# A hybrid encoder layer on one core: other DRAM layouts for operands, VectorE statistics for four tiles, a scheduling hint for the MLP residual, the last shifts on VectorE

## The chip, the cores and the metric

The kernel runs on one core of a Trainium2 chip. Five engines work side by side, each through its own queue in order: TensorE (PE, with its weight loads PEld), VectorE (DVE), ScalarE (ACT), GpSimd (POOL) and SyncE (SP, which here only issues DMAs). The metric is the device time of one execution in microseconds, lower is better.

## The reference, cut to what matters

One layer on 1024 tokens of 1024 channels, float32 in and out:

```
x   = layer_norm(x)
h   = x @ w_in                                   # 1024 x 3600
o_gdn = gated_delta(conv(h_qkv), decay, beta)    # chunked scan, both directions
o_na  = neighborhood_attention(q, k, v, rpb)     # 8 heads of 64, window 8 x 16, bias per offset
mix = concat(o_gdn, rms_norm(o_na)) @ w_out
x   = layer_norm(alpha * x + mix) * g1 + b1
ff  = square(relu(x @ w1 + b1)) @ w2 + b2        # 1024 -> 4096 -> 1024
out = layer_norm(alpha * x + ff) * g2 + b2'
```

## The kernel before, in words

Tokens are held as 8 tiles of 128. Each float32 matrix product is split into a high and a low part and takes three matmuls (hi x hi, hi x lo, lo x hi); the splits are a copy on ACT (or DVE) and a subtraction on DVE, the helper at L71. The program runs in stages:

- 0 to 60 us: x is loaded and normalised, the first projections start. Up to 400 us: the remaining w_in projections (`load_w`, one 512 KB column block of 128 channels per load), convolution and the delta-rule scan; 400 to 490 us: the projections of the attention heads (`na_v`, `na_qk`), woven with the last scan steps. `na_v` writes the values to a DRAM scratch `vs_d`.
- 490 to 680 us: attention, head by head. It loads queries and keys (L700, L704), values (`load_v`, L694, tile `vt`) and the position bias (`load_b`, L709, tile `B`). The scores are the matmuls `pss` (L735, L736); DVE adds the bias and takes the row maximum (`sn`, `nm`, L739); ACT takes the exponential; PE transposes and multiplies by the values (`po`, L754). In this stretch the queue of SP also loads the output weights (`woraw`) and the residual rows (`yacc`, L832).
- 680 to 715 us: the last part of the output projection (`psop`, L802 to L804). DVE adds it to `yacc` (L806 with a row sum, L809 without), `layer_norm` (L933 to L947) normalises each tile and stores it to the scratch `y_d`, PE transposes it (`psx`, L977) and ACT evacuates it (`x1f`, L981). The tiles go in two halves, `hf` 0 and 1, of four each.
- 715 to 1036 us: the upper MLP product by a Strassen-like scheme (`up_pair`, one pair of 128-column blocks g per call, products `psA`, `psB`, `psD`, ...). In it the weight sums of the second product are made as well: `w2_load` and `w2_sums` (L1033 to L1043) read w2 in 256 KB pieces, form four sums on DVE and store them to `t_d`. The activations and their sums go to `h_d` (256 KB per block, issued by ACT).
- 1036 to 1346 us: the lower MLP product, 7 products of 4 groups. For group n, `down_ops(n)` loads 1 MB of a left operand (`h_d`) and 1 MB of a right one (`t_d` or w2) into `d2r` (or `wraw` for every third n), and splits them by ACT L1184 and DVE L71. It is called two groups ahead of the matmuls `psdn` (`down_mm`, L1283 to L1285).
- `residual` (L1203 to L1210), called at group n = 1, loads the rows of `y_d` into `yr` and scales them. `take` adds the products to `yr`, and `finish` (L1220 to L1248) makes the last LayerNorm: tiles 4 to 7 in the middle of the seventh part, tiles 0 to 3 at the end, with `kind` 0 (tiles 0, 1), 1 (tile 2) or 2 (tile 3).

A scheduler sets the order of each engine's queue from its own estimate of the program, so one edit can move instructions far from it. Every hardware DMA of SP and ACT takes one of eight semaphores in turn, so it also waits until the eighth DMA before it, on either queue, has landed. `tc.issue_after(i)`, which the change uses, tells the scheduler to place an instruction behind `i`.

Of the kernel before, what the change touches and what calls it, by code (L numbers as in the profile page):

```python
# [15 lines left out]
P = 128  # L16
# [20 lines left out]
def tile_trunk(ctx: ExitStack, tc: tile.TileContext, A: dict, out: bass.AP):  # L37
# [378 lines left out]
    def decay_beta():  # L416
        wab_raw = p1.tile([P, NK, 16], F32, name="wab_raw")
        D.dma_start(wab_raw, A["w_in"][:, 2048:2064].rearrange("(kt p) c -> p kt c", p=P))
        wab = p1.tile([P, NK, 32], F32R, tag="iX", name="wab")
# [198 lines left out]
    ks_d = dr.tile([8, 2, 64, T], F32, name="ks_d")  # L618
    vs_d = dr.tile([4, 16, 32, 8, 64], F32, name="vs_d")
    starts = (0, 8, 24, 32)  # L620
    pace = pacer(steps, 300, 4)

    def na_qk(kind, p):
        hi, lo = load_w(2064 + (0 if kind == "q" else 512) + p * P, V)
        dst = qs_d if kind == "q" else ks_d
# [19 lines left out]
    def na_v(p):  # L645
        hi, lo = load_w(2064 + 1024 + p * P, V)
        for half in range(2):
            psj = ps_j("psv")
            gemm_x(psj, hi, lo, half, pace)
            vT = np_.tile([P, 512], F32, tag="nst", name="vT", bufs=4)  # L650
            S.activation(vT, psj, AF.Copy)
            ps = ps_j("pvt", (P, 4, P))
            for q in range(4):
                TE.transpose(ps[:, q], vT[:, q * P:(q + 1) * P], ident)
            st = np_.tile([P, 4, P], F32, tag="vst", name="vst", bufs=2)
            V.tensor_copy(st, ps)
            for e2 in range(2):
                for j in range(4):
                    p0 = e2 * 64 + starts[j]
                    D.dma_start(  # L660
                        vs_d[j, half * 8 + e2:half * 8 + e2 + 7:2, :, 2 * p:2 * p + 2, :]
                        .rearrange("r c h x -> c r (h x)"),
                        st[p0:p0 + 32])

# [226 lines left out]
    def w1_raw(g):  # L891
        raw = raw8().rearrange("p a (k c) -> p (a k) c", c=2 * P)
        D.dma_start(raw, A["w1"][:, g * 2 * P:(g + 1) * 2 * P].rearrange("(kt p) c -> p kt c", p=P))
        return raw

    def w_quad(raw, a, k):
        return raw[:, k * 4:k * 4 + 4, a * P:(a + 1) * P]

# [131 lines left out]
    def w2_load(g, hc):  # L1030
        r = w2p.tile([P, 2, 2, 256], F32, tag="r", name="w2r", bufs=2)
        for k in range(2):
            D.dma_start(r[:, k], A["w2"][(2 * g + k) * P:(2 * g + k + 1) * P, :]  # L1033
                        .rearrange("p (j c) -> p j c", j=2)[:, :, hc * 256:hc * 256 + 256])
        return r

    def w2_sums(g, hc, r):
# [24 lines left out]
    def up_pair(g, mid=None):  # L1062
# [58 lines left out]
        def join5(pe):  # L1121
            V.tensor_tensor(h22, u3, pe, ALU.add)  # L1122
            V.tensor_tensor(u2, u2, pe, ALU.add)
            act2(h22, h22, f + 1, h_d[2, g])
            step()
# [33 lines left out]
        for i, h in enumerate((s1, s2, s3, s4)):  # L1159
            S.dma_start(h_d[3 + i, g], h)  # L1160


    w2q = A["w2"].rearrange("(g k p) (j c) -> k j p g c", k=2, j=2, p=P)
    left = [h_d[i].rearrange("g p c -> p g c") for i in range(7)]
    right = [t_d[i].rearrange("g p c -> p g c") for i in range(4)]
    order = [(left[0], w2q[0, 0]), (left[4], right[1]), (left[5], right[2]), (left[3], right[0]),
# [53 lines left out]
    def finish(t, kind):  # L1220
# [16 lines left out]
        parts = ((0, 512), (512, 256), (768, 256)) if kind == 2 else ((0, 512), (512, 512))  # L1237
# [17 lines left out]
    def take(i, q, ps):  # L1255
# [19 lines left out]
        elif i == 5:  # L1275
            add(y0[:, lo_], y0[:, lo_], ps)
            stats(q, 0, 512)

    def down_mm(ps, n, q, c, start, stop):
        h, w = ops2[n]  # L1280
        qs_ = slice(q * P, (q + 1) * P)
        for k in range(4):
            TE.matmul(ps, h[:, 0, k, qs_], w[:, 0, k, c], start=(start and k == 0), stop=False)  # L1283
            TE.matmul(ps, h[:, 0, k, qs_], w[:, 1, k, c], start=False, stop=False)  # L1284
            TE.matmul(ps, h[:, 1, k, qs_], w[:, 0, k, c], start=False, stop=(stop and k == 3))  # L1285

# [37 lines left out]
def prepare(inputs):  # L1324
# [32 lines left out]
    def col(x, n):  # L1357
        return C(x.reshape(n, P).T)

    gb = [np.broadcast_to(a[k][0][:, None, :], (2, 8, 4)).reshape(64) for k in ("dt_bias", "a_log")]  # L1360
    d = {
# [5 lines left out]
        "ln_in_b": a["ln_in_b"].reshape(1, DM),  # L1367
        "w_in": a["w_in"][0],
# [4 lines left out]
        "rpbT": C(tab[:, idx]),  # L1373
        "w_out": a["w_out"][0],
# [29 lines left out]
```

## Time and profile before

| what | value |
|---|---|
| median of 3 runs | 1366.89 us (1367.37, 1366.89, 1360.23) |
| profiled execution | 1359.64 us, its span 1357.9 us |
| PE busy | 1288.7 us (95%) |
| DVE / ACT / POOL busy | 933.3 (69%) / 647.0 (48%) / 188.6 us (14%) |
| granted TensorE clock | 0.981 of full speed |
| DMA | 242690 packets, 268.32 MB, 198 GB/s over the span |
| packets under 512 B / 2 KB / 8 KB | 38928 / 171920 / 242592 |

The span runs from the first to the last instruction; the 1.7 us that the execution took beyond it lie around it. PE busy counts matmuls with modelled ends, so that 95% says how often PE had one to do, not how fast it was.

### The profile page before, as it was taken

How to read it: one execution, taken by the hardware profiler on the slowest of the kernel's cores; microseconds unless marked ns; L12 is line 12 of the kernel's file. 1: busy time of each engine (PE TensorE's matmuls, PEld its weight loads, DVE VectorE, ACT ScalarE, POOL GpSimd, SP SyncE). 2: the span in 40 equal slices, each digit the busy share in tenths (PEclk: the TensorE clock that was granted, in tenths of full speed). 3: DMA queues.
4: the chain of work that ended last, by engine and by line, in shares of the span. 5: the costliest groups of instructions: out<-in, count | busy, mean ns of one | idle time of the engine just before them, and what ended most of it. 6: DMA issues, size and time to landing. Idle time of an engine off the chain costs nothing.

```text
span 1357.9 us, 20075 instructions
## 1 busy us (share of the span) xinstructions
PE 1288.7 (95%) x7318; PEld 1073.8 (79%) x7318; DVE 933.3 (69%) x1707; ACT 647.0 (48%) x1256; POOL 188.6 (14%) x216
## 2 busy tenths in 40 slices
PE   5999999999999987899989899999999999999996
PEld 3688888887889876788867788888887888888885
DVE  6755797852247835757659988878885695565856
ACT  5457666433433136345487465445454533333532
POOL 3000001011103316913230000000000000000403
PEclk8999999998999998999998999999999999999998
DMA  6224638466877499955154786787779955556621
GB/s 196 52 82 125 157 102 170 134 156 185 254 214 218 138 263 319 244 167 154 51 180 146 226 298 218 266 286 254 251 268 379 379 196 187 190 185 219 252 83 63
DMA packets 242690, 268.32 MB, mean 198 GB/s; under 512 B 38928, under 2 KB 171920, under 8 KB 242592
## 3 DMA queue, kind: packets, MB, share of 16 engines
q1 hardware_dynamic: 208416, 216.70, 52.4%
q10 hardware_dynamic: 34176, 50.34, 10.6%
q8 instruction: 58, 0.95, 0.3%
q14 instruction: 40, 0.33, 0.1%
HBM read 181.99 MB, written 85.00 MB: 197 GB/s over the span
## 4 chain that ended last, share of the span: by engine, by line
PE 58%; DVE 5%; DMA 3%; ACT 2%; issue 1%; POOL 1%; SPq 0%; DVEq 0%; ACTq 0%
PE psdn L1283 7%; PE psdn L1284 7%; PE psdn L1285 7%; PE po L754 2%; PE psop L802 2%; PE psop L803 2%; PE psop L804 2%; PE psA L931 2%; PE psA L929 2%; PE psA L930 2%; PE psD L929 1%; PE psD L931 1%; PE psD L930 1%; PE psB L929 1%; PE psB L931 1%; PE psB L930 1%
## 5 line engine op out<-in xcount | busy, mean ns | idle before, releaser
L1283 PE MATMUL psdn<-d,d 128*128 128x512 f32 (+1 forms) x464 | 175.6, 385 | 2.9 <-ACT d L1184 2.9
L1284 PE MATMUL psdn<-d,d 128*128 128x512 f32 (+1 forms) x464 | 176.9, 382 | 0.0
L1285 PE MATMUL psdn<-d,d 128*128 128x512 f32 (+1 forms) x464 | 176.9, 382 | 0.0
L71 DVE TENSOR_TENSOR d<-d2r,d 128x1024 fp32r<-128x1024 f32 x72 | 85.9, 1239 | 65.3 <-ACT d L1184 60.6
L1184 ACT ACTIVATE d<-d2r 128x1024 fp32r<-128x1024 f32 x72 | 71.3, 1049 | 115.6 <-PE psdn L1285 92.9
L1283 PEld LDWEIGHTS psdn<-d,d 128*128 128x128 f32 x464 | 87.8, 190 | 20.4 <-ACT d L1184 3.3
L1285 PEld LDWEIGHTS psdn<-d,d 128*128 128x128 f32 x464 | 87.4, 188 | 17.1
L1284 PEld LDWEIGHTS psdn<-d,d 128*128 128x128 f32 x464 | 87.5, 189 | 16.8
L93 POOL TENSOR_TENSOR lrs<-lrs,mhalf 128x1 f32<-128x1 f32 x8 | 6.5, 808 | 600.7 <-DMA d2r<-h_d 546.3
L120 PE MATMUL psj<-xlo,whi 128*128 128x512 f32 x192 | 77.6, 404 | 2.6 <-DVE xlo L71 2.6
L119 PE MATMUL psj<-xhi,whi 128*128 128x512 f32 x192 | 77.0, 402 | 0.7 <-DVE xhi L170 0.7
L121 PE MATMUL psj<-xhi,wlo 128*128 128x512 f32 x192 | 76.5, 399 | 0.0
L71 DVE TENSOR_TENSOR d<-wraw,d 128x1024 fp32r<-128x1024 f32 x40 | 47.8, 1234 | 27.7 <-ACT d L1184 27.7
L71 DVE TENSOR_TENSOR wlo<-wraw,whi 128x1024 fp32r<-128x1024 f32 x28 | 34.2, 1223 | 46.6 <-ACT whi L110 41.9
L240 DVE SCALAR_TENSOR_TENSOR cy<-hraw,convw,cy 128x1024 f32<-128x1024 f32 x48 | 61.2, 1280 | 5.6 <-ACT cy L238 4.5
L887 ACT ACTIVATE w1t<-ws 128x512 fp32r<-128x512 f32 x64 | 39.6, 627 | 52.4 <-PE psE L931 7.8
L1057 ACT ACTIVATE h<-h,b1T 128x512 f32<-128x512 f32 x48 | 34.6, 720 | 62.9 <-DVE h L1122 31.2
L1184 ACT ACTIVATE d<-wraw 128x1024 fp32r<-128x1024 f32 x40 | 39.9, 1048 | 49.4 <-PE psdn L1285 41.5
L754 PEld LDWEIGHTS po<-vt,et 128*128 128x128 f32 x384 | 51.5, 195 | 9.0 <-ACT et L752 3.5
L754 PE MATMUL po<-vt,et 128*128 128x64 f32 x384 | 50.7, 271 | 5.7 <-ACT et L752 2.9
L743 ACT ACTIVATE ex<-sn,nm 128x384 f32<-128x384 f32 x64 | 39.0, 610 | 32.3 <-DVE nm L739 11.4
L931 PE MATMUL psA<-x,w1t 128*128 128x512 f32 x128 | 51.1, 400 | 1.8 <-DVE w1t L71 1.8
(344 smaller groups left out, 3488.5 us busy)
## 6 DMA issues: line engine op xcount, KB each, us to landing
wraw<-in_w_dram SPq DMA_DIRECT2D x21, 1024.0 KB, 8.1
d2r<-h_d SPq DMA_DIRECT2D x18, 1024.0 KB, 5.5
w2r<-in_w_dram SPq DMA_DIRECT2D x64, 256.0 KB, 5.0
t_d<-w2s ACTq DMA_DIRECT2D x32, 512.0 KB, 4.6
h_d<-hs ACTq DMA_DIRECT2D x64, 256.0 KB, 5.1
wraw<-in_w_in_dram SPq DMA_DIRECT2D x28, 512.0 KB, 4.6
h_d<-h ACTq DMA_DIRECT2D x48, 256.0 KB, 4.9
d2r<-t_d SPq DMA_DIRECT2D x11, 1024.0 KB, 7.7
```

The lines of the kernel that those rows point to most:

```text
L71: return eng.tensor_tensor(lo, full, f32(hi), ALU.subtract)
L119: pace(TE.matmul(ps, hi[:, kt], xhi[:, kt, sl], start=(kt == 0), stop=False))
L120: pace(TE.matmul(ps, hi[:, kt], xlo[:, kt, sl], start=False, stop=False))
L121: pace(TE.matmul(ps, lo[:, kt], xhi[:, kt, sl], start=False, stop=(kt == NK - 1)))
L240: V.scalar_tensor_tensor(y, raw[:, i:i + T], convw[:, ci, i:i + 1], y, ALU.mult, ALU.add)
L754: mm = TE.matmul(po[:, j], et[:, c], vts[j][:, t + c, e * 64:e * 64 + 64], start=(c == 0), stop=(c == 2))
L929: pace(TE.matmul(ps, w[:, 0, kt], x[:, 0, kt], start=(first and kt == 0), stop=False, skip_group_check=not first))
L931: pace(TE.matmul(ps, w[:, 1, kt], x[:, 0, kt], start=False, stop=(kt == 3), skip_group_check=not first))
L1184: S.activation(t[:, 0, k], raw[:, k], AF.Copy)
L1283: TE.matmul(ps, h[:, 0, k, qs_], w[:, 0, k, c], start=(start and k == 0), stop=False)
L1284: TE.matmul(ps, h[:, 0, k, qs_], w[:, 1, k, c], start=False, stop=False)
L1285: TE.matmul(ps, h[:, 1, k, qs_], w[:, 0, k, c], start=False, stop=(stop and k == 3))
```

## The change

It has four parts.

1. **DRAM layouts.** The host arranges w_in, w1, w2 and the position bias so that what one load takes for one partition is contiguous, and the scratch tensors `vs_d`, `h_d`, `t_d` are laid out by partition. The contiguous run of one partition becomes: w_in 512 B to 4 KB; the decay columns of w_in 64 B to 512 B; `vs_d` stores 512 B to 1 KB and loads 512 B to 2 KB; bias 1.5 KB to 4.5 KB; w1 1 KB to 4 KB (its first pieces `w1q` 512 B to 2 KB); `w2r` 1 KB to 2 KB; loads of `h_d`, `t_d` and w2 in the lower product 2 KB to 8 KB. A store to `h_d` was one contiguous 256 KB; it is now 128 runs of 2 KB, 32 KB apart. Stores to `t_d` keep runs of 1 KB. Numbers of bytes stay.
2. **VectorE statistics for tiles 4 to 7** in the first `layer_norm`: two BN_STATS and a BN_AGGR on DVE in place of a row sum in the addition and two Square passes on ACT, and the normalisation itself by one DVE tensor_scalar in place of an ACT pass.
3. **The MLP residual**: its loads are wrapped in `tc.issue_after` of the last matmul issued.
4. **The end**: for tiles 0 to 3 the shift by `b2L` is made on DVE, not on POOL; tile 2 is finished as tiles 0 and 1 are; tile 3 has no ACT and POOL passes left.

```diff
 def load_w:
-        D.dma_start(raw, A["w_in"][:, c0:c0 + P].rearrange("(kt p) c -> p kt c", p=P))
+        D.dma_start(raw, A["w_inB"][c0 // P])
 ...
-    vs_d = dr.tile([4, 16, 32, 8, 64], F32, name="vs_d")
+    vs_d = dr.tile([4, 4, 4, 32, 4, P], F32, name="vs_d")
 def load_v:
-            D.dma_start(v2[:, j % 2], vs_d[j].rearrange("(g r) c h x -> (r c) g (h x)", g=4)[:, :, p * P:p * P + P])
+            D.dma_start(v2[:, j % 2], vs_d[p, j].rearrange("r c g x -> (r c) g x"))
 def load_b:
-        loads.append(D.dma_start(B, A["rpbT"][h, t].rearrange("v q k -> q v k")))
+        loads.append(D.dma_start(B, A["rpbT"][h, t]))
 ...
-    h_d = dr.tile([7, NG, P, 512], F32, name="h_d")
-    t_d = dr.tile([4, NG, P, 512], F32, name="t_d")
+    h_d = dr.tile([7, P, NG, 512], F32, name="h_d")
+    t_d = dr.tile([4, P, NG, 512], F32, name="t_d")
 def layer_norm(t, sm, pool):
+        if sm is None:
+            st = pool.tile([P, 2, 6], F32, tag="lst", name="lst", bufs=2)
+            for c in range(2):
+                V.bn_stats(out=st[:, c, :], in_=yacc[t][:, c * 512:(c + 1) * 512])
+            mv = pool.tile([P, 2], F32, tag="lmv", name="lmv", bufs=2)
+            V.bn_aggr(out=mv, in_=st)
 ...
+            G.tensor_scalar_add(ve, mv[:, 1:2], LN_EPS)
+            rsqrt(rs[:, 0:1], ve, 1)
+            V.tensor_scalar(yacc[t], yacc[t], mv[:, 0:1], rs[:, 0:1], ALU.subtract, ALU.mult)
+            S.dma_start(y_d[t], yacc[t])
+            return
 ...
-            sm = wk.tile([P, 2], F32, tag="lsm", name="lsm", bufs=2)
+            sm = None if hf else wk.tile([P, 2], F32, tag="lsm", name="lsm", bufs=2)
 def w2_load:
-            D.dma_start(r[:, k], A["w2"][(2 * g + k) * P:(2 * g + k + 1) * P, :]
-                        .rearrange("p (j c) -> p j c", j=2)[:, :, hc * 256:hc * 256 + 256])
+            D.dma_start(r[:, k], A["w2R"][hc, 2 * g + k])
 ...
-            S.dma_start(h_d[3 + i, g], h)
+            S.dma_start(h_d[3 + i, :, g], h)
 def residual:
         for t, y in enumerate(yr):
-            D.dma_start(y, y_d[t])
+            with tc.issue_after(seam[0].ins):
+                D.dma_start(y, y_d[t])
 def finish:
-        if kind == 0:
+        if kind < 2:
 ...
-                G.tensor_tensor(yv[:, c], yv[:, c], b2L[:, c], ALU.add)
+                (V if t < 4 else G).tensor_tensor(yv[:, c], yv[:, c], b2L[:, c], ALU.add)
 ...
-            if kind == 2 and c0 < 768:
-                V.scalar_tensor_tensor(yv[:, c], yv[:, c], rs[:, 0:1], b2L[:, c], ALU.mult, ALU.add)
-            else:
-                S.activation(yv[:, c], yv[:, c], AF.Copy, scale=rs[:, 0:1])
-                G.tensor_tensor(yv[:, c], yv[:, c], b2L[:, c], ALU.add)
+            V.scalar_tensor_tensor(yv[:, c], yv[:, c], rs[:, 0:1], b2L[:, c], ALU.mult, ALU.add)
 def down_mm:
+            seam[:] = [TE.matmul(ps, h[:, 1, k, qs_], w[:, 0, k, c], start=False, stop=(stop and k == 3))]
```

Up to the last part of the output projection the engines issue the same instructions in the same order as before. From there on the order differs.

On VectorE, at the statistics of the last tiles of the first LayerNorm; before it reads (tiles 5 to 7, L806 is the addition with the row sum in two rows, L935 the mean):

```order
L806 ISA yacc,lsm<-yacc,psop 128x512
L806 ISA lsm 128x1
L935 TENSOR_SCALAR lnm<-lsm 128x1
L806 ISA yacc,lsm<-yacc,psop 128x512
L806 ISA lsm 128x1
L806 ISA yacc,lsm<-yacc,psop 128x512
L806 ISA lsm 128x1
L935 TENSOR_SCALAR lnm<-lsm 128x1
L806 ISA yacc,lsm<-yacc,psop 128x512
L806 ISA lsm 128x1
L958 CAST x_7083<-x1f 128x512
```

and with the change (L808 is the plain addition, L943 the normalisation of a tile):

```order
L808 TENSOR_TENSOR yacc<-yacc,psop 128x512
L943 TENSOR_SCALAR yacc<-yacc,lmv,lrs 128x1024
L936 BN_STATS lst<-yacc 128x6
L808 TENSOR_TENSOR yacc<-yacc,psop 128x512
L938 BN_AGGR lmv<-lst 128x2
L936 BN_STATS lst<-yacc 128x6
L808 TENSOR_TENSOR yacc<-yacc,psop 128x512
L970 CAST x_7083<-x1f 128x512
L71 TENSOR_TENSOR x_7083<-x1f,x_7083 128x512
L943 TENSOR_SCALAR yacc<-yacc,lmv,lrs 128x1024
L936 BN_STATS lst<-yacc 128x6
```

The statistics and the normalisation now stand between the additions that empty the PSUM tiles `psop`, and the first splits of the transposed first half have come ahead of the last additions.

On ScalarE at the same place, first before, where the evacuations `x1f` (L981) stand among the Square passes (`jk`, L939) and the normalisations (L946):

```order
L946 ACTIVATE yacc<-yacc,lrs 128x1024
L981 ACTIVATE x1f<-psx_7249,l1b,l1g 128x512
L981 ACTIVATE x1f<-psx_7258,l1b,l1g 128x512
L939 ACTIVATE jk,lsq<-yacc,lnm 128x512
L947 DMA y_d<-yacc 128x1024
L946 ACTIVATE yacc<-yacc,lrs 128x1024
L939 ACTIVATE jk,lsq<-yacc,lnm 128x512
L956 ACTIVATE x_7083<-x1f 128x512
L981 ACTIVATE x1f<-psx_7267,l1b,l1g 128x512
```

and with the change:

```order
L958 ACTIVATE yacc<-yacc,lrs 128x1024
L959 DMA y_d<-yacc 128x1024
L993 ACTIVATE x1f<-psx_7249,l1b,l1g 128x512
L944 DMA y_d<-yacc 128x1024
L993 ACTIVATE x1f<-psx_7258,l1b,l1g 128x512
L968 ACTIVATE x_7083<-x1f 128x512
L993 ACTIVATE x1f<-psx_7267,l1b,l1g 128x512
L968 ACTIVATE x_7083<-x1f 128x512
L993 ACTIVATE x1f<-psx_7276,l1b,l1g 128x512
```

The evacuations of the first half now follow one another, with only their own splits (L968) between them.

On SyncE, at the change from the upper to the lower MLP product, before (`yr` are the residual rows, `d2r` and `wraw` operands of the lower product):

```order
L1208 DMA yr<-y_d 128x1024 x6
L1181 DMA d2r<-h_d 128x4x512
L1181 DMA d2r<-in_w_dram 128x4x512
L1208 DMA yr<-y_d 128x1024
L1181 DMA wraw<-h_d 128x4x512
L1181 DMA wraw<-in_w_dram 128x4x512
L1181 DMA d2r<-h_d 128x4x512
L1181 DMA d2r<-in_w_dram 128x4x512
L1208 DMA yr<-y_d 128x1024
```

and with the change:

```order
L1221 DMA yr<-y_d 128x1024 x6
L1192 DMA d2r<-h_d 128x2048
L1192 DMA d2r<-in_w2Q_dram 128x2048
L1221 DMA yr<-y_d 128x1024
L1192 DMA wraw<-h_d 128x2048
L1192 DMA d2r<-h_d 128x2048
L1192 DMA d2r<-in_w2Q_dram 128x2048
L1192 DMA wraw<-in_w2Q_dram 128x2048
L1221 DMA yr<-y_d 128x1024
```

The residual loads stand where they stood; the right operand of group 3 (`wraw` from w2) has gone behind the two loads of group 2.

## Rows read from the trace of the kernel before

**Rows 1.** The page, the chain that ended last: shares by engine

```profile
PE 58%; DVE 5%; DMA 3%; ACT 2%; issue 1%; POOL 1%; SPq 0%; DVEq 0%; ACTq 0%
```

**Rows 2.** Stretches: us; PE, PEld, DVE, ACT, POOL busy (x); clock, DMA share, GB/s

```profile
60.00:400.00 340.00, 336.75 (x2613) 279.73 (x2611) 208.85 (x411) 177.85 (x474) 28.40 (x50) 0.99 0.58 155
...
500.00:560.00 60.00, 46.44 (x266) 40.24 (x267) 33.85 (x69) 31.79 (x62) 38.18 (x19) 0.91 1.05 306
...
680.00:740.00 60.00, 52.05 (x237) 41.27 (x236) 45.48 (x106) 49.56 (x91) 11.41 (x32) 0.89 0.56 184
740.00:800.00 60.00, 56.15 (x238) 45.30 (x237) 59.27 (x107) 32.42 (x57) 0.00 (x0) 0.97 0.67 215
800.00:1040.00 240.00, 240.00 (x1049) 196.51 (x1048) 191.58 (x348) 121.08 (x200) 0.00 (x0) 1.00 0.81 271
...
1045.00:1050.00 5.00, 2.08 (x10) 1.43 (x9) 0.26 (x1) 1.34 (x2) 0.00 (x0) 0.96 1.05 394
...
1100.00:1300.00 200.00, 200.00 (x884) 165.68 (x883) 133.60 (x150) 76.19 (x80) 15.92 (x12) 1.00 0.60 210
```

**Rows 3.** What PE waited for, 490 to 565 us: total us, times, longest us

```profile
PE pss L735 <- DVE nm L739: 12.1, 6, 7.1
```

**Rows 4.** Timeline, 515 to 530 us: start, us, instruction, idle before it

```profile
525.49 0.56 DVE L739 CUSTOM_DVE_ANT_0 sn<-pss,B 128x384 f32<-128x384 f32 x1 [5.17 <-DMA B<-in_rpbT_dram]
```

**Rows 5.** What PE waited for, 690 to 760 us

```profile
PE psx L977 <- ACT x1f L981: 6.1, 3, 3.1
PE psB L929 <- DVE p L1086: 3.9, 1, 3.9
```

**Rows 6.** What ACT waited for, 1040 to 1060 us

```profile
ACT d L1184 <- DMA wraw<-h_d: 5.7, 1, 5.7
```

**Rows 7.** Timeline of the end

```profile
1340.50 1.24 DVE L1229 SCALAR_TENSOR_TENSOR lrs<-lmv,lrs 128x1 f32<-128x1 f32 x1 [1.69 <-POOL lrs L93]
1341.66 0.68 DVE L1253 TENSOR_TENSOR yr<-yr,psdn 128x512 f32<-128x512 f32 x1
...
1345.73 0.28 PE L1285 MATMUL psdn<-d,d 128*128 128x256 f32 x1
...
1352.60 1.64 DVE L1244 SCALAR_TENSOR_TENSOR yr<-yr,lrs,b2L 128x512 f32<-128x512 f32 x2
```

**Rows 8.** Two stretches as in rows 2: values landed, then yacc and the bias

```profile
500.30:502.90 2.60, 2.51 (x21) 2.54 (x22) 0.48 (x3) 0.00 (x0) 0.00 (x0) 1.00 1.01 314
...
520.40:525.40 5.00, 0.00 (x0) 0.00 (x0) 0.00 (x0) 2.11 (x2) 0.69 (x1) 0.85 1.05 391
```

**Rows 9.** Groups by line and form, 640 to 720 us: busy us, mean ns | idle before

```profile
L939 ACT ACTIVATE jk<-yacc,lnm 128x512 f32<-128x512 f32 x16 | 11.4, 715 | 2.4 <-DVE lnm L935 2.4
L806 DVE CUSTOM_DVE_ANT_0 yacc<-yacc,psop 128x512 f32<-128x512 f32 x16 | 11.0, 687 | 8.2 <-PE psop L804 8.2
L946 ACT ACTIVATE yacc<-yacc,lrs 128x1024 f32<-128x1024 f32 x8 | 9.9, 1232 | 0.0
```

**Rows 10.** Groups by line and form, 1040 to 1358 us

```profile
L1234 POOL TENSOR_TENSOR yr<-yr,b2L 128x512 f32<-128x512 f32 x12 | 18.9, 1584 | 13.5 <-DVE yr L1233 6.1 <-issue 3.9 <-DVE lrs L1225 3.0
...
L1217 DVE BATCH_NORM_STATS2 st<-yr 128x6 f32<-128x512 f32 x15 | 10.3, 688 | 0.2
L1209 DVE TENSOR_TENSOR yr<-yr,gB 128x1024 f32<-128x1024 f32 x8 | 9.2, 1217 | 0.0
...
L1240 DVE SCALAR_TENSOR_TENSOR yr<-yr,lmv,g2B 128x512 f32<-128x512 f32 x3 | 4.5, 1522 | 0.0
...
L1244 DVE SCALAR_TENSOR_TENSOR yr<-yr,lrs,b2L 128x512 f32<-128x512 f32 x1 | 0.8, 753 | 0.0
L1205 DVE TENSOR_SCALAR gB<-gB 128x1024 f32<-128x1024 f32 x1 | 0.7, 685 | 0.0
```

**Rows 11.** DMA issues of the page: count, KB each, median us to landing

```profile
h_d<-hs ACTq DMA_DIRECT2D x64, 256.0 KB, 5.1
...
h_d<-h ACTq DMA_DIRECT2D x48, 256.0 KB, 4.9
```

More of the change, by code (lines that the diff above doesn't have):

```diff
@@ L417, in decay_beta @@
         wab_raw = p1.tile([P, NK, 16], F32, name="wab_raw")
-        D.dma_start(wab_raw, A["w_in"][:, 2048:2064].rearrange("(kt p) c -> p kt c", p=P))
+        D.dma_start(wab_raw, A["w_ab"])
         wab = p1.tile([P, NK, 32], F32R, tag="iX", name="wab")
@@ L623, in na_qk @@
     def na_qk(kind, p):
-        hi, lo = load_w(2064 + (0 if kind == "q" else 512) + p * P, V)
+        hi, lo = load_w(2048 + (0 if kind == "q" else 512) + p * P, V)
         dst = qs_d if kind == "q" else ks_d
@@ L645, in na_v @@
     def na_v(p):
-        hi, lo = load_w(2064 + 1024 + p * P, V)
+        hi, lo = load_w(2048 + 1024 + p * P, V)
         for half in range(2):
@@ L654, in na_v @@
                 TE.transpose(ps[:, q], vT[:, q * P:(q + 1) * P], ident)
-            st = np_.tile([P, 4, P], F32, tag="vst", name="vst", bufs=2)
-            V.tensor_copy(st, ps)
+            st = np_.tile([P, 2, 2, P], F32, tag="vst", name="vst", bufs=2)
+            V.tensor_copy(st, ps.rearrange("p (g r) x -> p r g x", r=2))
             for e2 in range(2):
@@ L660, in na_v @@
                     D.dma_start(
-                        vs_d[j, half * 8 + e2:half * 8 + e2 + 7:2, :, 2 * p:2 * p + 2, :]
-                        .rearrange("r c h x -> c r (h x)"),
-                        st[p0:p0 + 32])
+                        vs_d[p, j, e2:e2 + 3:2, :, half * 2:half * 2 + 2].rearrange("r c g x -> c r (g x)"),
+                        st[p0:p0 + 32].rearrange("c r g x -> c r (g x)"))
     for p in range(4):
@@ L891, in w1_raw @@
     def w1_raw(g):
-        raw = raw8().rearrange("p a (k c) -> p (a k) c", c=2 * P)
-        D.dma_start(raw, A["w1"][:, g * 2 * P:(g + 1) * 2 * P].rearrange("(kt p) c -> p kt c", p=P))
+        raw = raw8().rearrange("p a (k c) -> p a k c", c=P)
+        D.dma_start(raw, A["w1B"][2 * g:2 * g + 2].rearrange("a p k c -> p a k c"))
         return raw
     def w_quad(raw, a, k):
-        return raw[:, k * 4:k * 4 + 4, a * P:(a + 1) * P]
+        return raw[:, a, k * 4:k * 4 + 4]
     def w_steps(raw, w):
@@ L933, in layer_norm @@
     def layer_norm(t, sm, pool):
+        if sm is None:
[4 more added lines that the diff above has]
+            V.bn_aggr(out=mv, in_=st)
+            ve = pool.tile([P, 1], F32, tag="lve", name="lve", bufs=2)
+            rs = pool.tile([P, 2], F32, tag="lrs", name="lrs", bufs=2)
+            G.tensor_scalar_add(ve, mv[:, 1:2], LN_EPS)
[3 more added lines that the diff above has]
+            return
         nm = pool.tile([P, 1], F32, tag="lnm", name="lnm", bufs=2)
@@ L1101, in p2 @@
                 prod(pa, w["12"], X["21"], False)
-            act2(h11, pa, f, h_d[0, g])
+            act2(h11, pa, f, h_d[0, :, g])
             step()
@@ L1108, in p4 @@
             V.tensor_tensor(h21, u3, pd, ALU.add)
-            act2(h21, h21, f + 1, h_d[1, g])
+            act2(h21, h21, f + 1, h_d[1, :, g])
             step()
@@ L1123, in join5 @@
             V.tensor_tensor(u2, u2, pe, ALU.add)
-            act2(h22, h22, f + 1, h_d[2, g])
+            act2(h22, h22, f + 1, h_d[2, :, g])
             step()
@@ L1159, in up_pair @@
         for i, h in enumerate((s1, s2, s3, s4)):
-            S.dma_start(h_d[3 + i, g], h)
-    w2q = A["w2"].rearrange("(g k p) (j c) -> k j p g c", k=2, j=2, p=P)
-    left = [h_d[i].rearrange("g p c -> p g c") for i in range(7)]
-    right = [t_d[i].rearrange("g p c -> p g c") for i in range(4)]
+            S.dma_start(h_d[3 + i, :, g], h)
+    w2q = A["w2Q"]
+    left = [h_d[i] for i in range(7)]
+    right = [t_d[i] for i in range(4)]
     order = [(left[0], w2q[0, 0]), (left[4], right[1]), (left[5], right[2]), (left[3], right[0]),
@@ L1207, in residual @@
         for t, y in enumerate(yr):
-            D.dma_start(y, y_d[t])
+            with tc.issue_after(seam[0].ins):
+                D.dma_start(y, y_d[t])
             V.tensor_tensor(y, y, gB, ALU.mult)
@@ L1233, in finish @@
                 V.tensor_tensor(yv[:, c], yv[:, c], g2B[:, c], ALU.mult)
-                G.tensor_tensor(yv[:, c], yv[:, c], b2L[:, c], ALU.add)
+                (V if t < 4 else G).tensor_tensor(yv[:, c], yv[:, c], b2L[:, c], ALU.add)
                 D.dma_start(out[t * P:(t + 1) * P, c], yv[:, c])
             return
-        parts = ((0, 512), (512, 256), (768, 256)) if kind == 2 else ((0, 512), (512, 512))
+        parts = ((0, 512), (512, 256), (768, 256))
         for c0, cn in parts:
@@ L1277, in take @@
             stats(q, 0, 512)
+    seam = []
     def down_mm(ps, n, q, c, start, stop):
@@ L1284, in down_mm @@
             TE.matmul(ps, h[:, 0, k, qs_], w[:, 1, k, c], start=False, stop=False)
-            TE.matmul(ps, h[:, 1, k, qs_], w[:, 0, k, c], start=False, stop=(stop and k == 3))
+            seam[:] = [TE.matmul(ps, h[:, 1, k, qs_], w[:, 0, k, c], start=False, stop=(stop and k == 3))]
     cuts = {q: ((0, 512),) for q in range(4)}
@@ L1358, in col, with blocks @@
         return C(x.reshape(n, P).T)
+    def blocks(w):
+        return w.reshape(-1, P, w.shape[1] // P, P).transpose(2, 1, 0, 3)
+    w_in, w2 = a["w_in"][0], a["w2"][0]
     gb = [np.broadcast_to(a[k][0][:, None, :], (2, 8, 4)).reshape(64) for k in ("dt_bias", "a_log")]
@@ L1367, in prepare @@
         "ln_in_b": a["ln_in_b"].reshape(1, DM),
-        "w_in": a["w_in"][0],
+        "w_inB": blocks(np.concatenate([w_in[:, :2048], w_in[:, 2064:]], axis=1)),
+        "w_ab": w_in[:, 2048:2064].reshape(NK, P, 16).transpose(1, 0, 2),
         "convT": C(a["conv_w"][0].reshape(5, 12, P).transpose(2, 1, 0).reshape(P, 60)),
@@ L1372, in prepare @@
         "na_gT": C(np.concatenate([a["na_norm_g"][0]] * 2).reshape(P, 1)),
-        "rpbT": C(tab[:, idx]),
+        "rpbT": C(tab[:, idx].transpose(0, 1, 3, 2, 4)),
         "w_out": a["w_out"][0],
@@ L1378, in prepare @@
         "ln1_b": a["ln1_b"][0].reshape(1, DM),
-        "w1": a["w1"][0],
+        "w1B": blocks(a["w1"][0]),
         "b1T": col(a["b1"][0], NF),
-        "w2": a["w2"][0],
+        "w2R": w2.reshape(NF, P, 2, 2, 256).transpose(3, 0, 1, 2, 4),
+        "w2Q": w2.reshape(NF // 2, 2, P, 2, 512).transpose(1, 3, 2, 0, 4),
         "b2": a["b2"][0].reshape(1, DM),
```

6 lines of the change are left out of this document (3 added, 3 removed).

## The prediction, made before the result was known

> **What bounds the kernel now.** I read the chain of waits first: 58% of it is PE and 5% DVE, 3% DMA, 2% ACT [rows 1]. So the end is set by PE, and only time in which PE has no matmul, or runs on the lower clock, can be won. The busy times by stretch say where that is [rows 2]: from 800 to 1040 and from 1100 to 1300 us PE is busy all the time, from 60 to 400 us 336.75 of 340. What the change saves in these stretches on DMA (share 0.58 to 0.81), DVE or ACT is hidden. Time is lost in four places:
>
> - 500 to 560 us: PE 46.44 of 60, while the DMA share is 1.05. PE waited 12.1 us for the row maximum `nm`, the longest time 7.1 us [rows 3]; the timeline shows that DVE itself had waited 5.17 us for the bias tile `B` to land [rows 4]. This stretch is bound by transfers.
> - 680 to 740 us: PE 52.05, clock 0.89, and 740 to 800: PE 56.15 with DVE busy 59.27. PE waited 6.1 us for the evacuations `x1f` on ACT and 3.9 for `p` on DVE [rows 5].
> - 1045 to 1050 us: PE 2.08 of 5, DMA share 1.05: ACT waited 5.7 us for a left operand, `wraw` from `h_d` [rows 6].
> - The end: the last matmul ends at 1346.0, DVE works 8 us longer, until 1354.2 [rows 7].
>
> **The change part by part.**
>
> *Longer runs, attention.* The values' loads move 256 KB in runs of 512 B, now 2 KB. In a stretch in which such loads landed the queues moved 314 GB/s at share 1.01; in one filled with 4 KB rows and the bias, 391 at 1.05 [rows 8]. 262 KB take 0.835 us at the one rate and 0.67 at the other: 0.165 us per load, 16 loads by 561 us, 2.6 us. The bias loads (590 KB, 1.5 KB to 4.5 KB) have no stretch of their own; between the two rates they could win up to 0.37 us each, and I take 0.15, since 1.5 KB is nearer to the fast row: six of them by then, 0.9 us. All of it lies in front of a `B` for which PE waits, so I put it on the path: −3.5 us. Least is −1 (only the eight value loads ahead of the `B` of 525 us, 1.3 us), most −5.5 (the bias at 0.37 and some clock back).
> The Trainium skill ("DMA: Bandwidth & Descriptors", Specifications) gives 512 B as the least transfer that reaches the line rate. By that the values would win nothing, and 2.6 us of the term would go; the two rates above do not agree with it.
>
> *Longer runs elsewhere.* Loads of w_in, w1, w2 and of the lower product's operands land in the stretches in which PE is full. Their cover is PE itself. In the first 60 us one or two loads could gate, −0.3 (0 to −0.5).
>
> *VectorE statistics.* Four tiles lose two Square passes of 0.715 and a normalisation of 1.232 on ACT [rows 9]: 4 x 2.66 = 10.6 us less on ACT, in front of which the evacuations queued. DVE gets per tile two BN_STATS of 0.688 and a normalisation over 1024 columns; the nearest row is a tensor_scalar of that shape, 0.685, the upper bound a tensor_tensor, 1.217 [rows 10]. I take 0.685, as it is the same kind of instruction. The aggregate stands against the mean that it replaces, the plain addition against L806 at 0.687. That is 2.06 per tile, 8.2 us in all (10.4 at the upper bound). Is it hidden? DVE was idle 14.5 us from 680 to 740 [rows 2], of which it waited 8.2 for `psop` [rows 9]; of those 8.2 something can be filled, the other 6.3 surely, as far as data are there. By the order one round of the weight sums (four passes over 256 columns, some 1.7 us) also moves behind this stretch. So 8.2 − 1.7 = 6.5 us go into 6.3 and part of 8.2: DVE reaches `p` no later. On the other side the 6.1 us for `x1f` go, for the evacuations no longer queue behind the passes. But what is late next is DVE: it is full from 740 on, so PE would get to its wait for `p` earlier and wait longer there. Of the 6.1 us I count 2, since the splits of `x1f` also start earlier on DVE: −2. Ends: −6 (all of the wait), +4 (10.4 less the 6.3).
>
> *The late residual.* The hint is given with a matmul, and the loads are SP's. By the order they stand where they stood, in front of the first operands of the lower product; so it does nothing by itself. What did move is one right operand of group 3 behind the loads of group 2. The gap at 1045 hangs on the left operand of group 3, which waits in a full queue (394 GB/s); a few per cent more rate is worth −0.5. Ends: −3 (the gap), +5 (the later stores of the weight sums fall into the full queue and push it on).
>
> *The end.* POOL's shifts take 1.58 us each, and while they run DVE's fused passes take 1.52 on the mean, against 0.753 for the one that ran after them [rows 10]. The addition of tile 2 stood behind a one-column pass that had waited 1.69 us for POOL and then took 1.24 [rows 7]. By the order, from that addition on DVE has 12 passes of 512 columns, 4 pairs of half ones and 5 short ones: 12 x 0.688 + 4 x 0.8 + 5 x 0.2 = 12.5 us. From 1341.66, as before, this would end at 1354.2 and win nothing; but the 1.24 shrinks to some 0.15, and up to 1.69 of waiting goes: −1.1 to −2.8, less what PE, which still makes tile 2's product then, allows. I take −0.7, with −2 and +0.7 (passes not faster than now, the reciprocal root on POOL late) as ends. PE's end is not moved.
> The Trainium skill ("GPSIMD Engine Reference", Specifications) says that GpSimd's access to SBUF is shared with VectorE and contends with its instructions that have two SBUF inputs; the row of 1.52 against 0.753 agrees.
>
> **Sum:** −3.5 − 0.3 − 2 − 0.5 − 0.7 = −7.0 us. On the profiled execution, 1359.64 (span 1357.9 and 1.7 around it), that is 1352.6. The three runs were 1360.23, 1366.89 and 1367.37: with the profiled one, two near 1360 and two near 1367. A median of the changed kernel can fall in either group, 1353 or 1360; I put it in between, at 1357.
>
> **Rivals.**
> (a) *The transfers were not on the path.* SP issues a load only when the eighth one before it has landed, so shorter transfers could merely wait elsewhere, for a free buffer; against that speaks a share of 1.05 throughout. Then the attention term is near 0: 1356.1 on the profiled scale.
> (b) *DVE becomes the bound of the LayerNorm stage.* Its additions empty `psop`, and statistics, normalisations and splits now stand between them; each normalisation waits for POOL's reciprocal root. If none of the 10.4 us is hidden and PE waits once per tile for a BN_STATS that stands ahead of its addition (4 x 0.688 = 2.8), the stage is 13.2 us longer where I have −2: 1359.6 + 13.2 − 5 = 1367.8, slower than before. It decides from where the added work exceeds the 6.3 us of other idle. For it: DVE at 59.27 of 60 behind the stage. Against: ACT's 10.6 us.
> (c) *The pitch of the scratch tensors.* Stores to `h_d` were contiguous and become 2 KB runs 32 KB apart; ACT issues 112 of 256 KB [rows 11]. That is at most 29.4 of the 65 MB of 800 to 1040 us (240 us at 271 GB/s), 45%. If they took 1.65 times as long, the share of 0.81 would be 0.81 x 1.29 = 1.05: 11 us too much for the stretch and some 5 more at the gap of 1045, 1359.6 − 7 + 16 = 1368.6. Below 1.5 times it costs nothing.
> The Trainium skill ("DMA: Bandwidth & Descriptors", Latency and other measured facts) reports tiles of 16 KiB per partition that fall from about 214 GB/s to 207 at a row pitch of 512 KiB and to 103 at 4 MiB; no run here shows it, and 32 KB lies far below.
> (d) *The residual does come late.* Then the gap at 1045 and what the clock costs behind it go too, some 4 us: 1348.6. Against it: the order.
> (e) *All 6.1 us for `x1f` come back:* 1348.6 as well.
>
> **Chances.** Forecast 0.48, (a) 0.15, (b) 0.10, (c) 0.07, (d) 0.07, (e) 0.13. What a measurement of this kernel can tell is about 0.5%, 6.8 us; the forecast lies on that line, so its chance is split, 0.27 faster and 0.21 no change. Faster: 0.27 + 0.07 + 0.13 = 0.47. Same: 0.21 + 0.15 = 0.36. Slower: 0.17. The range: from 1346, below (d) and (e) with a little of the group near 1360, to 1370, which holds (b) and (c) in the lower group and the forecast in the upper one with 10 us to spare. The forecast's own range is 1349 to 1363.
>
> **What would show it.** Right: the `B` for which PE waited at 525 lands 2 to 3 us earlier against the start of the stage; the waits for `x1f` are below 2 us while those for `p` grow; DVE is nearly full from 690 to 800; the residual rows are issued where they were, with a gap of PE of 2 to 4 us near 1045; POOL has no pass after the last matmul. Wrong: a DMA share above 0.9 in the upper product (c); waits of PE for `psop` on DVE (b); the residual's loads behind the first operands (d); the same landing times in attention (a).

## The result, and the profile after

The changed kernel is slower: 1369.43 us median of 20 runs against 1363.82 for the kernel before. Over all runs the ratio is 1.0052 with a 95% interval of 1.0032 to 1.0073: half a per cent, but clear of the noise. The forecast was 7 us faster. The profiled execution took 1364.96 us, its span 1363.2.

Four instants on TensorE cut the two executions into the same stages. The first fence is the timeline of PE before (start, us, instruction, idle before it): the first transposes of the LayerNorm stage, the end of the wait for `p`, and the end of the wait at the start of the lower product. The last matmul starts at 1345.73 [rows 7].

```profile
690.30 0.38 PE L977 MATMUL psx<-ident,yacc 128*128 128x128 f32 x2
...
758.87 0.47 PE L929 MATMUL psB<-xT,w1t 128*128 128x512 f32 x1 [3.85 <-DVE p L1086]
...
1049.76 0.80 PE L1283 MATMUL psdn<-d,d 128*128 128x512 f32 x1 [2.92 <-ACT d L1184]
```

The same and the last matmul in the timeline after:

```profile
683.62 0.38 PE L989 MATMUL psx<-ident,yacc 128*128 128x128 f32 x2
...
750.72 0.80 PE L928 MATMUL psB<-xT,w1t 128*128 128x512 f32 x1 [4.00 <-DVE p L1097]
...
1057.30 0.80 PE L1294 MATMUL psdn<-d,d 128*128 128x512 f32 x1 [13.05 <-ACT d L1195]
...
1353.15 0.28 PE L1296 MATMUL psdn<-d,d 128*128 128x256 f32 x1
```

From these, in us:

| stage | before | after | difference |
|---|---|---|---|
| start to first transposes | 690.3 | 683.6 | −6.7 |
| LayerNorm stage, to the end of the wait for `p` | 68.6 | 67.1 | −1.5 |
| upper product and the change to the lower one | 290.9 | 306.6 | +15.7 |
| lower product, to the start of the last matmul | 296.0 | 295.9 | −0.1 |
| end | 12.2 | 10.0 | −2.2 |

So in this pair of executions all that was forecast to be won was won by 750 us, and the change of products took twice that back. Busy times by stretch after, columns as in [rows 2]:

```profile
680.00:740.00 60.00, 56.04 (x266) 43.24 (x264) 56.21 (x109) 41.86 (x74) 7.59 (x20) 1.00 0.48 167
740.00:800.00 60.00, 52.20 (x210) 41.33 (x211) 56.60 (x103) 32.17 (x54) 0.00 (x0) 0.89 0.71 240
...
1030.00:1040.00 10.00, 8.24 (x37) 6.44 (x35) 0.99 (x3) 1.78 (x3) 0.00 (x0) 1.00 0.84 308
1040.00:1045.00 5.00, 3.03 (x12) 2.18 (x12) 3.48 (x7) 2.64 (x4) 0.00 (x0) 1.00 0.85 304
1045.00:1050.00 5.00, 0.00 (x0) 0.00 (x0) 2.51 (x3) 0.72 (x1) 0.00 (x0) 0.67 1.02 421
1050.00:1055.00 5.00, 0.00 (x0) 0.00 (x0) 0.00 (x0) 0.00 (x0) 0.00 (x0) 0.50 1.00 359
```

From 1045 to 1055 PE does nothing; from 1030 to 1040 DVE is busy 0.99 us of 10. How long DVE waited for its store of the weight sums from 1000 to 1060 us (total, times, longest), first before, then after:

```profile
DVE w2s L1039 <- DMA t_d<-w2s: 3.5, 1, 3.5
```

```profile
DVE w2s L1050 <- DMA t_d<-w2s: 14.3, 2, 9.2
```

The two long pieces in the chain of waits of that stretch after (start, us):

```profile
1027.28 11.71 DMA t_d<-w2s
...
1040.60 14.66 DMA t_d<-w2s
```

And ACT behind the second store (`ACTq` is its issue of DMAs):

```profile
1055.33 0.81 ACTq L1171 DMA_DIRECT2D h_d<-hs  x2
1056.19 4.85 ACT L1195 ACTIVATE d<-d2r 128x1024 fp32r<-128x1024 f32 x5 [10.47 <-DMA yr<-y_d]
```

The reader is to see a loop. The sums of w2 have one buffer `w2s`; DVE can't begin the next round until the store of the last one has landed. That store took 11.7 us, DVE stood, the last `psF` was not taken up, and ACT stood behind DVE. The second store took 14.7 us, and ACT, whose third store behind it had the same one of the eight semaphores, could not issue that one before; the operand splits for PE are behind that store on ACT's queue. (The last row names a load of residual rows as the releaser. It landed at 1055.45 us; the store's semaphore came free at 1055.26, and ACT issued at 1055.33.)

### The profile page after: what moved, and what is told of

It is laid out like the page before. It is cut to its first block, busy times and chain, and to the rows that moved or that the text cites. A ratio compares the mean times of both kernels' runs of the same rounds, so it can differ in the third digit from the quotient of the medians.

```text
span 1363.2 us, 20066 instructions
## 1 busy us (share of the span) xinstructions
PE 1289.6 (95%) x7318; PEld 1074.3 (79%) x7318; DVE 938.7 (69%) x1719; ACT 636.4 (47%) x1235; POOL 175.3 (13%) x201
## 5 line engine op out<-in xcount | busy, mean ns | idle before, releaser
L801 PE MATMUL psop<-wo,oh 128*128 128x512 f32 x128 | 52.5, 413 | 0.2 <-ACT oh L795 0.2
L803 PE MATMUL psop<-wo,ol 128*128 128x512 f32 x128 | 51.4, 404 | 0.0
```

The lines of the kernel that those rows point to most:

```text
L801: pace(TE.matmul(ps, oh[:, k], hi[k][:, c], start=(k == 0), stop=False))
L803: pace(TE.matmul(ps, ol[:, k], hi[k][:, c], start=False, stop=(k == nk - 1)))
```

## The experiments

In each, the time is given as a ratio to the kernel before on the same chip, with its 95% interval. "U" is the time from the end of the wait for `p` to the end of the last matmul: 587.1 us before, 602.7 after. It leaves out attention, which varies from run to run. It is read from one profiled execution of each kernel; the two kernels below that leave this stretch as it was before (attention layouts alone, the end alone) have 588.1 and 586.9, so a difference of 1 us in U says nothing.

**No statistics.** The changed kernel with

```diff
-            sm = None if hf else wk.tile([P, 2], F32, tag="lsm", name="lsm", bufs=2)
+            sm = wk.tile([P, 2], F32, tag="lsm", name="lsm", bufs=2)
```

> The changed kernel with the old statistics (row sums, Square passes on ACT) for all eight tiles; layouts, hint and end stay changed. Theory T1 (the statistics load VectorE where the scheduler otherwise fits rounds of the w2 sums, so the last rounds and their stores fall behind the residual rows at the change to the lower product, where VectorE and then ACT wait): the two gaps of PE near 1040 (2.98 and 13.05 us) shrink to at most 4 us together, attention and end keep their gains, 8 to 11 us faster than the kernel before. Theory T2 (stores to the re-pitched scratch are slow, so the queue is full there): the gaps stay above 12 us, 4 to 8 us slower than before. Theory T3 (the change of products is bound by transfers that cannot come earlier, so whatever is won earlier is waited for there): gap about 9 us, within 2 us of before.

Measured 1.0017 (0.9983 to 1.0051); U 591.6. The waits of PE from 1020 to 1062 us:

```profile
PE psdn L1294 <- ACT d L1195: 3.8, 1, 3.8
```

The gap is as T1 said, T2 falls, and T3 too (no 9 us). But the gain that T1 promised isn't there: U is 4.5 us longer than before, of which only 0.8 is in this gap. The LayerNorm stage took 72.6 us against 68.6 before: without the statistics the layouts make it 4 us longer. What DVE waited for there, 685 to 765 us:

```profile
DVE w2s L1050 <- DMA t_d<-w2s: 5.9, 2, 4.2
```

It is the same store, at another place; before, DVE waited for it 2.1 us there. So the order alone is not the whole cause.

**Old layout of the scratch.** `h_d` and `t_d` as before, all else changed (their stores and loads follow and are left out here):

```diff
-    h_d = dr.tile([7, P, NG, 512], F32, name="h_d")
-    t_d = dr.tile([4, P, NG, 512], F32, name="t_d")
+    h_d = dr.tile([7, NG, P, 512], F32, name="h_d")
+    t_d = dr.tile([4, NG, P, 512], F32, name="t_d")
```

> The changed kernel with h_d and t_d laid out as before (a store of 256 KB contiguous, loads in runs of 2 KB); all else changed. T1 and T3: the gaps near 1040 stay at 13 to 17 us, within 2 us of the changed kernel (5 to 8 us slower than before). T2: they fall to 4 us or less, 7 to 10 us faster than before.

Measured 1.0031 (1.0001 to 1.0061); U 602.5, as the changed kernel. T2, and with it rival (c) of the prediction, is refuted as the cause: without the 32 KB between the runs the loss stays. The edit also puts the loads of `h_d` and `t_d` back to runs of 2 KB, with w2 still at 8 KB; the last two stores of the sums still took 12.0 and 13.9 us.

**Residual really late.** The loads are tied to an instruction of their own queue, no longer to a matmul; in `down_ops`:

```diff
+            seam[:] = [D.dma_start(raw, src[:, sl])]
```

> The changed kernel, but the residual's loads are tied to the last operand load of group 3 (an instruction of the same queue) instead of a matmul, so that all eight stand behind the operands of groups 0 to 3. Eight loads of 512 KB are 4.2 MB, 10.7 us at 391 GB/s. T1: stores of the sums and operand loads have 10.7 us less in front of them; the gaps fall from 16 to 4 to 8 us, 1 to 5 us faster than before. T2: the queue stays slow, the gaps fall by less than 5 us. T3: as T1, since the same bytes leave the place; T1 and T3 are told apart by the others.

Measured 0.9947 (0.9915 to 0.9979), U 589.1, a gap of 4.0 us: 7 us faster than before instead of 1 to 5. The eight loads (4.2 MB) are part of what the stores stood beside. The last store still took 13.7 us here, but the one before it only 2.9, so that the last could be issued at 1027.4: a slow store costs time only where DVE and ACT stand behind it.

**Statistics alone**, on the kernel before.

> The kernel before with the VectorE statistics for tiles 4 to 7 alone. T1: the LayerNorm stage wins 1 to 2 us, the rounds move as in the changed kernel, gaps of 10 to 17 us near 1046, 8 to 13 us slower than before. T2: no pitch changed, gap about 3 us as before, 0 to 2 us faster. T3: gap about 4 us, same time as before.

Measured 1.0027 (0.9994 to 1.006); U 593.1, so +5.9. The LayerNorm stage took 66.5 us, 2.0 less than before, as forecast. None of the theories has the size: gaps of 7.7 us, less than T1's 10 and more than T3's 4. The last store of the sums took 8.4 us here, with the same place in the order as in the changed kernel, where it took 14.7:

```profile
1038.64 8.39 DMA t_d<-w2s
```

Statistics +5.9, layouts without statistics 591.6 − 587.1 = +4.5, both together +15.6: more than the sum of 10.4. That led to theory T4: the statistics put the last rounds late (by the order 30 of 32 rounds stand before the first operand split, 32 before the change), and the longer runs of the loads make every store in short runs slow.

**Short loads.** All operand loads of the lower product in 2 KB runs again: `h_d` and `t_d` as in the old layout, and w2 too (its line alone is shown).

```diff
-    w2q = A["w2Q"]
+    w2q = A["w2"].rearrange("(g k p) (j c) -> k j p g c", k=2, j=2, p=P)
```

> The changed kernel with every operand load of the lower product back in runs of 2 KB (h_d, t_d and w2 as before); w_in, values, bias, w1 and the pieces of w2 for the sums keep their long runs, statistics and end stay changed. Theory T4 (beside loads in runs of 8 KB a store in runs of 1 KB gets a smaller part of the queues, so the last stores of the sums land late, VectorE waits for their buffer and ACT behind it): the last store of sums, 14.2 us to land in the changed kernel, takes about 8 as with the statistics alone; PE's gaps near 1040 fall from 16 to about 8 us; 6 to 9 us faster than the changed kernel, 0 to 3 us faster than the one before. T1 alone (only the place of the rounds in the order counts): the order is the same, gaps stay at 14 to 17 us, 4 to 7 us slower than before.

Measured 0.9995 (0.9965 to 1.0024), U 597.3, gaps of 9.5 us. The stores in the chain:

```profile
1028.09 9.39 DMA t_d<-w2s
1039.10 9.85 DMA t_d<-w2s
```

DVE's instructions are the same in the same order as in the changed kernel, so T1 alone, which wanted gaps of 14 to 17 us, falls. T4 has the direction; the 5.4 us of U are a little less than its 6 to 9. From the old layout of the scratch this kernel differs in the loads of w2 alone: when they too have runs of 2 KB, U falls from 602.5 to 597.3 and the last store from 13.9 to 9.9 us.

**Long stores.** The changed kernel, with only `t_d` laid out so that a store writes 4 KB per partition:

```diff
-    t_d = dr.tile([4, P, NG, 512], F32, name="t_d")
+    t_d = dr.tile([P, NG, 2, 4, 256], F32, name="t_d")
-        S.dma_start(t_d[:, :, g, hc * 256:hc * 256 + 256].rearrange("i p c -> p i c"), t)
+        S.dma_start(t_d[:, g, hc].rearrange("p i c -> p (i c)"), t.rearrange("p i c -> p (i c)"))
-    right = [t_d[i] for i in range(4)]
+    right = [t_d[:, :, :, i] for i in range(4)]
```

> The changed kernel with t_d laid out so that a store of the sums writes one run of 4 KB per partition (its loads in the lower product then have runs of 1 KB); nothing else differs from the changed kernel. T4: the store has runs near those of the loads, its last landings fall from 11.3 and 14.2 us to 7 to 10, PE's gaps from 16 to 6 to 11 us, 4 to 9 us faster than the changed kernel; the loads in runs of 1 KB lie under a busy PE and cost nothing. T1 alone: the gaps stay at 14 to 17 us.

Measured 0.997 (0.994 to 1.0001), U 588.0: 14.7 of the 15.6 us are gone. DVE's instructions are the same in the same order; on ACT the shape of the stores differs, and three instructions changed places with a neighbour. So the place of the rounds in the order is excluded as the difference. The loads of `t_d`, now in runs of 1 KB, begin only behind the gap, at 1053.8 us. Chain and PE's waits of 1020 to 1062 us:

```profile
1029.83 5.28 DMA t_d<-w2s
```

```profile
PE psdn L1294 <- ACT d L1195: 2.9, 1, 2.9
```

The piece of 5.28 us is the last store but one, to be held against 11.71. The last one is no longer in the chain; it was issued at 1036.72 and landed at 1046.31, so it took 9.6 us against 14.66. The bytes of a store are the same, and while the last one was out the queues were as full. In the changed kernel and here (columns as in [rows 2]):

```profile
1040.60:1055.30 14.70, 3.03 (x12) 2.18 (x12) 5.42 (x7) 3.36 (x4) 0.00 (x0) 0.71 1.00 376
```

```profile
1036.70:1046.30 9.60, 9.60 (x44) 7.88 (x42) 3.24 (x5) 2.28 (x3) 0.00 (x0) 1.00 1.02 405
```

The stores get through earlier, and since each round waits for the store before it, the gain adds up: the last store but one was issued 3.1 us ahead of the first `d2r` load, in the changed kernel 1.2 us behind it. T4 holds for this place.

**Long stores and late residual.** The two edits together.

> As the run with long stores of the sums, and the residual's loads behind the operands of group 3 as in the run with the late residual (which had gaps of 4 us and was 0.53% faster than before). T4: the sums' stores no longer wait behind loads, gaps of 2 to 4 us, 7 to 10 us faster than before. T1: as the late residual alone, 6 to 8 us faster than before. The two overlap; the landing of the last store of sums (13.3 us with the late residual alone) tells them apart: below 10 by T4, 12 to 14 by T1.

Measured 0.9965 (0.993 to 1.0), U 589.0, gap 3.9 us. The last store of sums took 9.7 us (counted, as the 13.3, from the end of its issue), just inside T4's answer, but the time is not better than with either edit alone, so this run decides little. The last two stores of `h_d` activations, in 2 KB runs, now took 12.3 and 12.8 us, counted in the same way.

**Late residual alone**, on the kernel before.

> The kernel before with only the residual's loads tied to the last operand load of group 3. If those loads stood in front of the operands for which PE waits (2.92 us), the gap falls below 1.5 us and the time by 2 to 5 us. If the operands are late for another reason, gap and time stay within 1 us.

Measured 1.0055 (1.002 to 1.0089): a miss. The gap grew to 7.6 us. ACT from 1036 to 1062 us:

```profile
1043.93 11.37 ACTq L1160 DMA_DIRECT2D h_d<-hs  x2
1055.35 2.00 ACT L1185 ACTIVATE d<-d2r 128x1024 fp32r<-128x1024 f32 x2 [11.52 <-DMA d2r<-h_d]
```

With the residual gone from its place another DMA's semaphore came round for ACT's second store of `hs`: it was held by a load of group 2, issued at 1042.66 and landed at 1054.90, and ACT sat 11 us on it. What the residual's bytes cost in the kernel before was not tested cleanly by this.

**All three.** Short loads, long stores, late residual.

> The changed kernel with three edits that worked one by one: operand loads of the lower product in runs of 2 KB, stores of the sums in runs of 4 KB, the residual behind the operands of group 3. T4: the h_d stores (runs of 2 KB), which took 12.3 to 12.8 us beside loads of 8 KB in the run with long stores and the late residual, now take 6 to 9, PE's gap near 1040 falls from 3.9 to 1 to 2.5 us, 6 to 11 us faster than before. If the gap is set by the bytes in front of the operands and not by shares, it stays at 3.5 to 4.5.

Measured 0.992 (0.9886 to 0.9955), 1349.17 us median, U 584.3. It is 0.8% faster than the kernel before, the lowest ratio of all (its interval overlaps that of the late residual). PE's whole wait from 1000 to 1100 us:

```profile
PE psdn L1293 <- ACT d L1196: 0.2, 1, 0.2
```

The three last `h_d` stores of activations took 6.8 to 8.6 us from the end of their issue, inside T4's range.

**Long stores without statistics**, a second place for T4.

> The changed kernel with the old statistics and the long stores of the sums: T4 at a second place. Without the statistics the layouts made the LayerNorm stage (from the first transposes to the end of PE's wait for p) 72.6 us instead of 68.6, while VectorE waited 5.9 us there for the store of the sums (2.1 before). T4: that wait falls below 1.5 us and the stage to 67 to 69.5 us. If the layouts delay the stage otherwise (the w1 loads), it stays at 72 to 73.

Measured 0.9981 (0.9952 to 1.0011), U 586.7. The LayerNorm stage fell from 72.6 to 69.6 us, three of the four, and DVE's wait for the store from 5.9 to 3.3 us. The direction is T4's, the size is short of what it said.

**Attention layouts alone**, on the kernel before (`vs_d` and the bias).

> The kernel before with the new layouts of the values and of the position bias alone. If attention is bound by transfers as predicted: the stage up to the first transposes 2 to 5 us shorter and the time 2 to 5 us below before. If other loads and the free slots set the landing of the bias: within 1 us. Later stages as before (gap of 3 us near 1046).

Measured 0.997 (0.9938 to 1.0001), so not clear of no change; U 588.1, first transposes at 684.3 us, 6 us earlier than in the profile before. What PE waited for from 485 to 565 us, to be held against 12.1 [rows 3]:

```profile
PE pss L734 <- DVE nm L738: 6.0, 4, 3.3
```

**The end alone**, on the kernel before.

> The kernel before with the changed end alone. From the last matmul to the end of the span took 11.9 us before and 9.6 to 9.8 in all kernels with the changed end: 9.6 to 9.9 here, 1.5 to 2.5 us faster than before, if nothing else in the order moves; over 11 if the gain came from elsewhere.

Measured 0.9979 (0.9946 to 1.0012), so the time itself is not clear of no change. From the end of the last matmul to the end of the span it took 9.5 us (1343.83 to 1353.37) against 11.9: the expected gain, and 0.1 more.

## Why the prediction was wrong, point by point

**The step that failed** is the one on the late residual and the change of products: "−0.5. Ends: −3 (the gap), +5 (the later stores of the weight sums fall into the full queue and push it on)". The mechanism stood in the upper end, but as a store that makes the queue longer. It measured +15.7, since the store was itself what DVE and ACT waited for, and since the last two took 11.7 and 14.7 us where with longer runs they need 5.3 and 9.6. A second buffer for `w2s`, which would let DVE go on without the store, was not tried. The median of the changed kernel lies just inside the range that was given, up to 1370; that is luck, for the range reached so far for rivals (b) and (c), and neither came.

**A second step made that possible**: "Longer runs elsewhere [...] Their cover is PE itself." Their own landings were covered, as far as PE was busy 200.00 us of 200 from 820 to 1020 after, too. Not priced was what the longer runs do to stores that share the queues with them. Medians of the page after for the stores (those of `t_d` keep their runs; those of `h_d` were contiguous before):

```profile
t_d<-w2s ACTq DMA_DIRECT2D x32, 512.0 KB, 5.9
h_d<-hs ACTq DMA_DIRECT2D x64, 256.0 KB, 3.7
...
h_d<-h ACTq DMA_DIRECT2D x48, 256.0 KB, 6.1
```

On the page before they were 4.6, 5.1 and 4.9 (the last two in [rows 11]): two kinds of stores became slower and one quicker, so the medians alone decide nothing. The stores at the change of products do. The last two stores of the sums, in us from issue to landing:

| kernel | run of the store | runs of the loads of the lower product | last but one | last |
|---|---|---|---|---|
| statistics alone | 1 KB | 2 KB | 8.7 | 8.4 |
| short loads | 1 KB | 2 KB | 9.4 | 9.9 |
| old layout of the scratch | 1 KB | 2 KB, w2 8 KB | 12.0 | 13.9 |
| changed kernel | 1 KB | 8 KB | 11.7 | 14.7 |
| long stores | 4 KB | 8 KB | 5.3 | 9.6 |

With the late residual, where the order is another, the last one took 13.7 (1 KB beside 8 KB), 10.1 (4 KB beside 8 KB) and 8.6 (4 KB beside 2 KB). The Trainium skill ("DMA: Bandwidth & Descriptors", Queues, rings and completion order) says that each DMA engine takes turns between the queues with work, a packet of some descriptors at a time. By that rule, as an estimate with equally many descriptors a turn, the bytes would be shared as the run lengths: 1 to 8 for the changed kernel, 1 to 2 with long stores or with short loads; the order of the last stores agrees. The two queues while the last store was out in the changed kernel, loads (`q1`) and stores (`q10`), with packets, MB and share (a packet of the profile is one run here; 512 of those on `q10` are the store's, of 1 KB):

```profile
q1 hardware_dynamic: 720, 4.72, 84.8%
q10 hardware_dynamic: 669, 0.80, 14.9%
```

About as many packets of either queue, but six times the bytes of the loads. With short loads it was 1206 packets against 613, not as many. So that the turns are the mechanism no run here shows; the dependence on both run lengths the table does show.

**The moved round.** "one round of the weight sums [...] also moves behind this stretch" was booked as 1.7 us less work for DVE. I did not ask where the rounds come out: two of 32 stand behind the first operand split. The trace before had the wait already. Of the 6.3 us of DVE that the prediction counted as free from 680 to 740 us, 5.2 were waits of these sums, 2.1 of them for the store:

```profile
DVE w2s L1039 <- DMA t_d<-w2s: 2.1, 1, 2.1
```

**The LayerNorm stage** was forecast at −2 and measured −1.5 here and −2.0 with the statistics alone. Against the changed kernel without statistics (72.6 us) they are worth 5.5, for there the layouts cost 4. What PE waited for after, 683 to 753 us, against [rows 5]:

```profile
PE psB L929 <- DVE xT L71: 5.0, 2, 3.2
PE psB L928 <- DVE p L1097: 4.0, 1, 4.0
PE psx L989 <- ACT x1f L993: 1.0, 2, 0.5
```

The wait for `x1f` fell from 6.1 to 1.0 us, and DVE (56.21 of 60 from 680 to 740) took 5.0 back, as said; but in the splits `xT`, not at `p`, where the wait stayed at 4.0. Rival (b) did not come. The normalisation took 0.808 us, between the bounds and nearer to the one chosen.

**Attention** was forecast at −3.5; to the first transposes the pair of profiles shows −6.7, and the kernel with these layouts alone −6.0, with a ratio whose interval just touches 1. But over all profiles the instant lies at 686.1 to 692.4 us with the old layouts (four) and at 683.6 to 694.4 with the new (ten), on the mean 689.2 and 687.7; so the −6.7 of the pair is in good part chance. PE's first long wait behind the bias was 7.1 to 7.4 us with the old layouts and 3.3 to 6.5 with the new; the second, near 555 us, was 1.7 to 2.0 us with the old layouts and 1.1 to 9.4 with the new. Rival (a) is not supported by the first wait; why the second is at times so long, and what the layouts are worth on the mean, stays open.

**The end** was forecast at −0.7 and measured about −2.2. Right mechanism, wrong size: the sum had the passes at their time without POOL, but took too much off for PE. After, 1300 to 1364 us, the passes were as quick as that:

```profile
L1247 DVE TENSOR_TENSOR yr<-yr,b2L 128x512 f32<-128x512 f32 x6 | 4.0, 676 | 0.0
...
L1253 DVE SCALAR_TENSOR_TENSOR yr<-yr,lmv,g2B 128x512 f32<-128x512 f32 x1 | 0.7, 741 | 0.0
```

And PE held DVE up by only 0.68 us before the last addition:

```profile
1353.47 0.42 DVE L1262 TENSOR_TENSOR yr<-yr,psdn 128x256 f32<-128x256 f32 x1 [0.68 <-PE psdn L1296]
```

Behind the last matmul DVE then worked 6.4 us, until 1359.8, against 8.2 before.

**That the residual does not come late** was right: its loads were issued from 1010.9 us on, six of the eight in front of the operands of group 1. What it would be worth was undersized at 4 us: 602.7 − 589.1 = 13.6 us of U in the changed kernel, for there the last store but one took 2.9 us instead of 11.7.

## What to carry to other kernels

When loads get longer runs, look at the stores that share the queues and keep their short ones: find who waits for them, and lengthen these first. A wait that is covered in one order is not covered in the next; when an edit adds work to a full engine, follow the filler work that the scheduler moves to the place where it comes out, and look there for a single buffer and a queue in which others stand behind it.

## What the runs showed of the hardware that was not expected

The last store of 512 KB took 14.7 us to land in runs of 1 KB and 9.6 in runs of 4 KB, the one before it 11.7 and 5.3; while the last one was out, the queues moved 376 and 405 GB/s. Stores of 2 KB runs 32 KB apart landed about as fast as contiguous ones (medians of 3.7 and 3.7 us for `hs`, 6.1 and 5.9 for `h`, changed kernel and old layout). In the pause of PE the granted clock was 0.67 of full speed on the mean from 1045 to 1050 us and 0.50 from 1050 to 1055, which is 1.2 GHz, the lower of its two levels.
